# One y visit per group of heads in a Mamba-2 layer, y kept in place of x, and a gate's half moved

## The chip, the cores and the metric

The kernel runs on one core of a Trainium2 chip. Its engines work in parallel, each through its own queue in order: PE (TensorE, matrix products into PSUM), ACT (ScalarE), DVE (VectorE), POOL (GpSimd) and SP (SyncE), which here only starts transfers (DMA). The metric is the device time of one execution in microseconds (us). The kernel before takes 1143.02 us, the median of three runs (1142.99, 1143.02 and 1146.43).

## The reference

The program is a two-layer decoder trunk on 256 positions of width 2048, in float32: a Mamba-2 layer (64 heads of 64 channels in 8 groups, state 128), shared keys and values, an attention layer, and norms. The change is in the Mamba-2 layer, cut to what matters:

```
z, xbc, dt = split(rmsnorm(x) @ w_in)              # xbc: x (4096), B (1024), C (1024)
x, B, C    = split(silu(conv4(xbc)))
dt         = softplus(dt + dt_bias);  a = dt * -exp(A_log)
decay      = exp(cumsum(a)[l] - cumsum(a)[s])  for s <= l      # per head
y          = (C B^T * decay) @ (x * dt)            # per head; C B^T per group
y          = y + D * x
out        = grouped_rmsnorm(y * silu(z)) @ w_out  # 8 groups of 512 channels
```

The sequence is one chunk of 256, so the state that is carried on is never read. After it come `kv = rmsnorm(x) @ w_kv`, 16 attention heads with rope and a causal softmax, and the last two projections.

## The kernel before, in words

All weights are used once. A *unit* is two slices of 128 input channels by 512 output columns of one weight (512 KB). SP loads it (`load`, L292), ACT rounds it to `hi`, DVE subtracts to get `lo` (`split`, L311), and PE multiplies it in `products` (L343) with activations that are split in the same way: for each of two halves of the 256 positions and each of two slices, three large products of 512 columns into a bank `ps`. That is 12 large products a unit and 4,624 in the program, 16 of them for dt. Loads run four units ahead, hi and lo three. `ORDER` (L34) is the order of the blocks of 512 columns: B, C, x and z of the input projection, `o` and `p` of the output projection. The attention layer's blocks follow.

Everything else is *side work*: Python generators that issue a few instructions and yield a condition or a time. After every few large products, `some` (L250, L154) lets generators go on whose inputs, by the planner's own clock (`Paced`, `Clock`, with a cost for each instruction), have been ready for `MARGIN` = 750 ns. So the position of a side product in PE's stream is fixed when the program is built. All instructions of PE, ACT and DVE are issued through one helper line, L126; in the profile they are told apart by tile names. Side products go to four banks `s`. I call a run of side products between two large ones a *visit*.

For a group g of 8 heads (4 head pairs, 512 channels):

- `x_evac` (L805) takes the finished x block out of PSUM. `turn` (L376) scales it by the row factor r0 on ACT, transposes it in 32x32 blocks on DVE into `T`, writes it to DRAM (`turned`, SP) and reads it back with channels in rows into `U` (four reads, POOL).
- `conv_gen` (L621) makes the convolved x in `xs` (12 DVE products, ACT's tanh) and, transposed by PE and multiplied by dt, `xd`.
- `pair_gen(g, j)` (L692), one for each pair j, takes an `em` tile, loads two rows of cumulative sums into all partitions (POOL, 256 KB, L698), makes the decay (ACT) and multiplies by the group's C B^T in `cb` (DVE). There are two `em` tiles. The generator of an odd pair then multiplies pairs j-1 and j on PE in one visit: per pair, four products of xd with em, two heads into the two halves of the bank's rows, so each uses 64 of PE's 128 columns. Each pair's generator then makes `yt` = D xs + q on DVE and multiplies it by 0.5 and by the gate z.
- `z_gen` (L783) makes z (1 + tanh(z/2)) from the turned z block, which was scaled by r0.
- `norm_gen` (L745) waits for the group's four pairs, makes the group's norm (ACT squares, two PE transposes, DVE) and the operand `yn` of the output projection.

Of the kernel before, what the change touches and what calls it, by code (L numbers as in the profile page):

```python
# [9 lines left out]
F32 = mybir.dt.float32  # L10
F32R = mybir.dt.float32r
I32 = mybir.dt.int32
AF = mybir.ActivationFunctionType
OP = mybir.AluOpType

P = 128
L = 256
# [152 lines left out]
def trunk_kernel(ctx: ExitStack, tc: tile.TileContext, x, a_norm_g, a_w_in, a_conv_w, a_conv_b,  # L170
# [3 lines left out]
    clock = Clock()  # L174
# [22 lines left out]
    PE = Paced(clock, nc.tensor, pe_cost, 0.0)  # L197
# [4 lines left out]
    def dram(t, offset, ap):  # L202
# [6 lines left out]
    psum = ctx.enter_context(tc.tile_pool(name="psum", bufs=1, space=bass.MemoryType.PSUM))  # L209
    scratch = ExitStack()  # L210
    work = scratch.enter_context(tc.tile_pool(name="ssd", bufs=2, reuse_waits="tile"))
    S = [Slots(work, {"T": ([P, 512], 2), "u": ([P, 4, L], 1), "xs": ([P, 4, L], 3), "xd": ([P, 2, 512], 1),
                      "cb": ([P, 384], 4), "em": ([P, 2, 384], 2), "z": ([P, 1024], 1), "yt": ([P, 4, L], 2)})]
    banks = Slots(psum, {"s": ([P, 512], 8 - MAIN_BANKS)}, clock.banks)
    spare = Parts(big, "U", "y5", [P, 1024], 2)
    B = {}
# [4 lines left out]
    def of(tag):  # L221
        return next(s for s in (banks, S[0], spare) if tag in s.shape)

    def can(*tags):
        return lambda: all(of(t).free(t) > 0 for t in tags)

    def take(tag):
        return of(tag).take(tag)
# [3 lines left out]
    def give(*tiles):  # L232

        for t in tiles:
            key = t.tensor.name, t.offset
            freed.append((next(s for s in (banks, S[0], spare) if key in s.held), key, clock.last))

# [163 lines left out]
    def by_channel(U):  # L401

        return U.rearrange("p (b j l) -> p j b l", b=8, j=4)
# [2 lines left out]
        return a.rearrange("p j (b l) -> p j b l", l=32)  # L406


    ga = const.tile([16, P], F32, name="ga")
    SP.dma_start(ga, dram(a_norm_g, 0, [[P, 16], [1, P]]))  # L410
    xl = [big.tile([P, D], F32, name=f"xl{t}", tag=f"y{4 + t}") for t in range(2)]
    xv = x[0].rearrange("(t p) d -> p t d", p=P)
# [53 lines left out]
    def root(t, count):  # L466

        v, h, y, a = (t[:, i, :] for i in range(4))
        DVE.tensor_scalar(v, v, 1.0 / count, EPS, op0=OP.mult, op1=OP.add)
        ACT.activation(h, v, AF.Sqrt)  # L470
        DVE.reciprocal(y, h)
        DVE.tensor_mul(a, y, y)
        DVE.tensor_mul(a, a, v)
        DVE.tensor_scalar(a, a, -0.5, 1.5, op0=OP.mult, op1=OP.add)
        DVE.tensor_mul(y, y, a)
# [22 lines left out]
    warm_up()  # L498
    nt = const.tile([P, 4, 2], F32, name="r0")
    r0 = nt[:, 2, :]  # L500

    def squares(h):

# [4 lines left out]
    def first_norm():  # L508
        DVE.tensor_reduce(nt[:, 0, :], ss, axis=mybir.AxisListType.X, op=OP.add)
        root(nt, D)  # L510

    gv = const.tile([P, 112], F32, name="gv")
    cbias = const.tile([P, 48], F32, name="cbias")
# [34 lines left out]
    st = {}  # L548
# [28 lines left out]
    def dt_gen(w):  # L577
        u, m, e, s, s2 = (w[0:64, i, :] for i in range(5))
        DVE.scalar_tensor_tensor(m, u, -1.0, u, op0=OP.mult, op1=OP.min)
        yield  # L580
        ACT.activation(e, m, AF.Exp)
        yield
        DVE.tensor_scalar(m, e, 2.0, None, op0=OP.add)
        DVE.reciprocal(s2, m)
        DVE.tensor_mul(s, e, s2)
        yield
        DVE.tensor_mul(s2, s, s)
        DVE.tensor_scalar(m, s2, 1.0 / 17, None, op0=OP.mult)
        for n in range(7, 0, -1):
            DVE.scalar_tensor_tensor(m, m, 1.0 / (2 * n + 1), s2, op0=OP.add, op1=OP.mult)  # L590
            if n % 2:
                yield
        DVE.scalar_tensor_tensor(m, m, 1.0, s, op0=OP.add, op1=OP.mult)
        DVE.tensor_scalar(e, u, 0.0, None, op0=OP.max)
        dt = s2
        DVE.scalar_tensor_tensor(dt, m, 2.0, e, op0=OP.mult, op1=OP.add)
        yield
        a, b = m, e
        DVE.tensor_scalar(b, dt, negA, None, op0=OP.mult)
        POOL.memset(u, 1.0)  # L600
        yield
        DVE.tensor_tensor_scan(a, u, b, 0.0, OP.mult, OP.add)
        yield
        AC = hbm.tile([64, L], F32, name="AC")
        POOL.dma_start(AC, a)
        st["AC"] = AC
        b = w[:, 2, :]
        DVE.tensor_copy(b[64:128, :], a)
        DVE.tensor_copy(b[0:64, :], dt)
        yield DVE.ns + 3000.0  # L610
        yield can("s")
        p = take("s")[:, :L].rearrange("p (t c) -> p t c", t=2)
        for t in range(2):
            PE.transpose(p[:, t, :], b[:, t * P:(t + 1) * P], ident)
        yield
        dal = const.tile([P, 2, P], F32, name="dal", tag="c2")
        ACT.activation(dal, p, AF.Copy)
        give(p)
        st["dal"] = dal
# [69 lines left out]
                side.add(cb_gen(q), lambda: ("B", q) in st and ("C", q) in st)  # L689
        return evac  # L690

    def pair_gen(g, j):  # L692

        c = 4 * g + j
        E = take("em")
        AC = st["AC"]
        R = bass.AP(tensor=AC.tensor, offset=AC.offset + 2 * c * L, ap=[[0, P], [L, 2], [1, L]])
        POOL.dma_start(E[:, :, :L], R)  # L698
        yield copied(E)
        yield lambda: "dal" in st  # L700
        dal = st["dal"]
        for h in range(2):
            a = 64 + 2 * c + h
            ACT.activation(E[:, h, 256:384], E[:, h, P:L], AF.Relu, bias=dal[:, 1, a:a + 1], scale=-1.0)
            ACT.activation(E[:, h, 0:256], E[:, h, 0:256], AF.Relu, bias=dal[:, 0, a:a + 1], scale=-1.0)
        ACT.activation(E, E, AF.Exp, scale=-1.0)
        yield lambda: ("cb", g) in st
        DVE.tensor_mul(E, E, st["cb", g][:, None, :].to_broadcast([P, 2, 384]))
        st["em", g, j], when["em", g, j] = E, clock.last
        if j % 2:  # L710
            yield lambda: ("xd", g) in st and ("em", g, j - 1) in st
            yield max(when["xd", g], when["em", g, j - 1])
            yield lambda: of("s").free("s") > 1 and (("y", g) in st or can("yt")())
            for i in (j - 1, j):
                xd, E, q = st["xd", g], st.pop(("em", g, i)), take("s")[:, :L]
                for h in range(2):
                    PE.matmul(q[h * 64:(h + 1) * 64, :], lhsT=xd[:, 0, i * P + h * 64:i * P + (h + 1) * 64],
                              rhs=E[:, h, 0:256], start=True, stop=False)
                for h in range(2):
                    PE.matmul(q[h * 64:(h + 1) * 64, P:L], lhsT=xd[:, 1, i * P + h * 64:i * P + (h + 1) * 64],  # L720
                              rhs=E[:, h, 256:384], start=False, stop=True)
                give(E)
                st["q", g, i], when["q", g, i] = q, clock.last
            if ("y", g) not in st:
                st["y", g], st["n", g] = take("yt"), 0
            yield
        else:
            yield lambda: ("q", g, j) in st
            yield when["q", g, j]
        xd, xs, q = st["xd", g], st["xs", g], st.pop(("q", g, j))  # L730
        y = st["y", g][:, j, :]
        DVE.scalar_tensor_tensor(y, xs[:, j, :], Dv[:, c:c + 1], q, op0=OP.mult, op1=OP.add)
        give(q)
        st["x", g] = st.get(("x", g), 0) + 1
        if st["x", g] == 4:
            give(xs, xd, st["cb", g])
        yield lambda: ("z", g) in st
        z = st["z", g]
        y = y.rearrange("p (b l) -> p b l", l=32)
        DVE.scalar_tensor_tensor(y, y, 0.5, by_channel(z)[:, j], op0=OP.mult, op1=OP.mult)  # L740
        st["n", g] += 1
        if st["n", g] == 4 and g not in (1, 3):
            give(z)

    def norm_gen(g):  # L745
# [37 lines left out]
    def z_gen(U, there, g):  # L783

        yield there
        if g in (1, 3):
            yield lambda: g == 1 or st.get(("n", 1)) == 4
            z = big.tile([P, 1024], F32, name=f"z{g}", tag="y4")
        else:
            yield can("z")  # L790
            z = take("z")
        ACT.activation(z, U, AF.Tanh, scale=0.5)
        yield
        DVE.scalar_tensor_tensor(z, z, 1.0, U, op0=OP.add, op1=OP.mult)
        give(U)
        st["z", g] = z

    def z_evac(g):
        def evac(ps, t):
            U, there = turn(ps, t, r0)  # L800
            if t:
                side.add(z_gen(U, there, g))
        return evac

    def x_evac(g):  # L805
        base = conv_evac(4 * g, ("xs", g), g)

        def evac(ps, t):
            base(ps, t)
            if not t:  # L810
                return
            for j in range(4):
                side.add(pair_gen(g, j), lambda: "AC" in st and can("em")())
            side.add(norm_gen(g), lambda: st.get(("n", g)) == 4)
        return evac

# [66 lines left out]
    def r1_gen():  # L883
# [16 lines left out]
        ACT.activation(rB, R, AF.Copy)  # L900
        give(R)
        yield
        csr = const.tile([P, 2, L], F32, name="csr", tag="c2")
        DVE.tensor_mul(csr, B["cs"], rB[:, None, :].to_broadcast([P, 2, L]))
        B["csr"] = csr
        bop = [big.tile([P, 4, 2 * L], F32R, name=f"bop{i}", tag=f"y{i}") for i in range(4)]
# [341 lines left out]
```

## Time and profile before

| | |
|---|---|
| median of the runs | 1143.02 us |
| profiled execution, its own time | 1143.61 us |
| its span, first to last instruction | 1141.9 us |
| PE busy | 1130.1 us, 99%, 5217 instructions |
| DVE busy | 839.2 us, 73%, 1283 instructions |
| ACT busy | 641.6 us, 56%, 890 instructions |
| POOL busy | 124.4 us, 11%, 217 instructions |
| HBM traffic | 226 GB/s over the span |

Shares are of the span. Matmuls are pipelined: the recorded time of one overlaps the next, so PE's rate is read from starts and not from durations. A wait is told as the engine that waited, the tile that it worked for, and what ended the wait. An fp32 side product is recorded as two instructions (two passes); a large product, whose operands are rounded, as one.

### The profile page before, as it was taken

How to read it: one execution, taken by the hardware profiler on the slowest of the kernel's cores; microseconds unless marked ns; L12 is line 12 of the kernel's file. 1: busy time of each engine (PE TensorE's matmuls, PEld its weight loads, DVE VectorE, ACT ScalarE, POOL GpSimd, SP SyncE). 2: the span in 40 equal slices, each digit the busy share in tenths (PEclk: the TensorE clock that was granted, in tenths of full speed). 3: DMA queues.
4: the chain of work that ended last, by engine and by line, in shares of the span. 5: the costliest groups of instructions: out<-in, count | busy, mean ns of one | idle time of the engine just before them, and what ended most of it. 6: DMA issues, size and time to landing. Idle time of an engine off the chain costs nothing.

```text
span 1141.9 us, 14900 instructions
## 1 busy us (share of the span) xinstructions
PE 1130.1 (99%) x5217; PEld 923.2 (81%) x5217; DVE 839.2 (73%) x1283; ACT 641.6 (56%) x890; POOL 124.4 (11%) x217
## 2 busy tenths in 40 slices
PE   9999999999999999999999999999999999999996
PEld 6888888888888888888878888888888888888885
DVE  5787878778799878787877558876445597887564
ACT  5666566767656666667554655434343444445353
POOL 2011112012011111101000000000000012122000
PEclk9999999999999999999999999999999999999998
DMA  8787888878778777777765467768658688888852
GB/s 263 222 242 242 249 229 278 268 243 253 210 222 240 223 237 225 237 234 231 215 232 177 162 197 218 224 200 261 220 174 244 209 248 237 263 250 261 254 185 92
DMA packets 130363, 258.91 MB, mean 227 GB/s; under 512 B 12976, under 2 KB 13824, under 8 KB 129904
## 3 DMA queue, kind: packets, MB, share of 16 engines
q1 hardware_dynamic: 119232, 226.01, 63.2%
q0 software_dynamic: 11056, 31.95, 10.9%
q8 instruction: 41, 0.67, 0.2%
q14 instruction: 34, 0.28, 0.1%
HBM read 235.83 MB, written 22.09 MB: 226 GB/s over the span
## 4 chain that ended last, share of the span: by engine, by line
PE 96%; DMA 1%; DVE 1%; ACT 0%; SPq 0%; issue 0%; ACTq 0%; DVEq 0%
PE ps L126 90%; PE s L126 6%; DMA raw<-in_a_w_in_dram 1%; PE ps_dt L126 0%; DVE xs L126 0%; DVE lo L126 0%; ACT hi L126 0%; SPq L416 0%; DVE x L126 0%; DVE T L126 0%; SPq L306 0%; ACT T L126 0%; ACT x L126 0%; DVE sfin L126 0%; ACTq L1243 0%
## 5 line engine op out<-in xcount | busy, mean ns | idle before, releaser
L126 DVE TENSOR_TENSOR lo<-raw,hi 128x1024 fp32r<-128x1024 f32 (+1 forms) x385 | 462.7, 1215 | 192.1 <-ACT hi L126 189.1
L126 ACT ACTIVATE hi<-raw 128x1024 fp32r<-128x1024 f32 (+1 forms) x385 | 397.7, 1052 | 263.3 <-PE ps L126 137.5
L126 PE MATMUL ps<-hi,hT 128*128 128x512 f32 x1280 | 401.1, 394 | 0.5 <-ACT hi L126 0.4
L126 PEld LDWEIGHTS ps<-hi,hT 128*128 128x128 f32 x1280 | 235.6, 188 | 49.2 <-issue 2.1
L126 PE MATMUL ps<-lo,hT 128*128 128x512 f32 x640 | 249.8, 390 | 0.0
L126 PE MATMUL ps<-hi,bop 128*128 128x512 f32 x512 | 161.1, 396 | 0.0
L126 PE MATMUL ps<-hi,yn 128*128 128x512 f32 x512 | 159.7, 393 | 0.0
L126 PE MATMUL ps<-hi,kvop 128*128 128x512 f32 x512 | 158.2, 390 | 0.0
L397 POOL DMA_DIRECT2D U<-turned x128 | 74.3, 587 | 748.9 <-DMA turned<-T 408.2
L126 PEld LDWEIGHTS ps<-lo,hT 128*128 128x128 f32 x640 | 120.1, 188 | 26.4 <-DVE lo L126 0.9
L126 PEld LDWEIGHTS ps<-hi,kvop 128*128 128x128 f32 x512 | 95.7, 188 | 19.7
L126 PEld LDWEIGHTS ps<-hi,bop 128*128 128x128 f32 x512 | 95.8, 188 | 19.4
L126 PEld LDWEIGHTS ps<-hi,yn 128*128 128x128 f32 x512 | 94.7, 188 | 19.4 <-issue 0.5
L126 PE MATMUL ps<-lo,yn 128*128 128x512 f32 x256 | 99.8, 390 | 0.0
L126 PE MATMUL ps<-lo,bop 128*128 128x512 f32 x256 | 99.8, 390 | 0.0
L126 PE MATMUL ps<-lo,kvop 128*128 128x512 f32 x256 | 99.7, 389 | 0.0
L126 PE MATMUL ps<-hi,oop 128*128 128x512 f32 x256 | 78.9, 390 | 0.0
L126 DVE STREAM_TRANSPOSE T<-ps 128x512 f32<-128x512 f32 x64 | 43.4, 699 | 25.6 <-ACT ps L126 15.9
L126 DVE SCALAR_TENSOR_TENSOR xs<-u,cw,xs 128x255 f32<-128x255 f32 (+2 forms) x144 | 59.7, 475 | 0.0
L126 ACT ACTIVATE em<-em,dal 128x128 f32<-128x128 f32 (+1 forms) x128 | 54.4, 449 | 5.0 <-DMA em<-AC 2.9
L126 PEld LDWEIGHTS ps<-lo,bop 128*128 128x128 f32 x256 | 48.0, 188 | 10.3
L126 PEld LDWEIGHTS ps<-lo,yn 128*128 128x128 f32 x256 | 48.0, 188 | 10.1
(165 smaller groups left out, 922.5 us busy)
## 6 DMA issues: line engine op xcount, KB each, us to landing
raw<-in_a_w_in_dram SPq DMA_DIRECT2D x159, 512.0 KB, 5.3
raw<-in_a_w_out_dram SPq DMA_DIRECT2D x64, 512.0 KB, 4.8
raw<-in_w_kv_dram SPq DMA_DIRECT2D x64, 512.0 KB, 4.8
raw<-in_b_w_in_dram SPq DMA_DIRECT2D x64, 512.0 KB, 4.7
turned<-T SPq DMA_DIRECT2D x64, 256.0 KB, 4.3
U<-turned POOLq DMA_DIRECT2D x128, 128.0 KB, 6.5
raw<-in_b_w_out_dram SPq DMA_DIRECT2D x32, 512.0 KB, 4.9
em<-AC POOLq DMA_DIRECT2D x32, 256.0 KB, 6.0
```

Source lines behind the costliest of these rows:

```text
L126: return call(out, *args, **kw)
L397: POOL.dma_start(U[32 * q:32 * q + 32].rearrange("p (b c) -> p b c", b=8), src)
```

## The change

`pair_gen` is cut in two. `em_gen(g, j)` makes one pair's em tile; `y_gen(g)` waits for xd and all four em tiles and issues the products of all four pairs in one visit, two pairs to a bank, side by side. y is then written over the group's xs, so `yt` is gone, and its room goes to a fourth xs and two more em tiles (four in all). The product with z is done for two pairs at once and without the factor 0.5; that factor is now in r0h = r0/2, by which z is scaled when it leaves PSUM, and z's tanh loses its scale of 0.5. Three small tiles change places.

```diff
-    S = [Slots(work, {"T": ([P, 512], 2), "u": ([P, 4, L], 1), "xs": ([P, 4, L], 3), "xd": ([P, 2, 512], 1),
-                      "cb": ([P, 384], 4), "em": ([P, 2, 384], 2), "z": ([P, 1024], 1), "yt": ([P, 4, L], 2)})]
+    S = [Slots(work, {"T": ([P, 512], 2), "u": ([P, 4, L], 1), "xs": ([P, 4, L], 4), "xd": ([P, 2, 512], 1),
+                      "cb": ([P, 384], 4), "em": ([P, 2, 384], 4), "z": ([P, 1024], 1)})]
...
+        DVE.tensor_scalar(r0h, r0, 0.5, None, op0=OP.mult)
...
-    def pair_gen(g, j):
+    def em_gen(g, j):
...
         DVE.tensor_mul(E, E, st["cb", g][:, None, :].to_broadcast([P, 2, 384]))
         st["em", g, j], when["em", g, j] = E, clock.last
-        if j % 2:
-            yield lambda: ("xd", g) in st and ("em", g, j - 1) in st
-            yield max(when["xd", g], when["em", g, j - 1])
-            yield lambda: of("s").free("s") > 1 and (("y", g) in st or can("yt")())
-            for i in (j - 1, j):
-                xd, E, q = st["xd", g], st.pop(("em", g, i)), take("s")[:, :L]
+        st["ems", g] = st.get(("ems", g), 0) + 1
+        if st["ems", g] == 4:
+            give(st["cb", g])
+
+    def y_gen(g):
+
+        yield lambda: ("xd", g) in st and st.get(("ems", g)) == 4
+        yield max(when["xd", g], *(when["em", g, j] for j in range(4)))
+        yield lambda: of("s").free("s") > 1
+        xd, y = st["xd", g], st["xs", g]
+        Q = []
+        for i in (0, 2):
+            q = take("s").rearrange("p (j l) -> p j l", j=2)
+            Q.append(q)
+            for j in (i, i + 1):
+                E = st.pop(("em", g, j))
                 for h in range(2):
-                    PE.matmul(q[h * 64:(h + 1) * 64, :], lhsT=xd[:, 0, i * P + h * 64:i * P + (h + 1) * 64],
+                    PE.matmul(q[h * 64:(h + 1) * 64, j - i, :], lhsT=xd[:, 0, j * P + h * 64:j * P + (h + 1) * 64],
                               rhs=E[:, h, 0:256], start=True, stop=False)
                 for h in range(2):
-                    PE.matmul(q[h * 64:(h + 1) * 64, P:L], lhsT=xd[:, 1, i * P + h * 64:i * P + (h + 1) * 64],
+                    PE.matmul(q[h * 64:(h + 1) * 64, j - i, P:L], lhsT=xd[:, 1, j * P + h * 64:j * P + (h + 1) * 64],
                               rhs=E[:, h, 256:384], start=False, stop=True)
                 give(E)
...
-        y = st["y", g][:, j, :]
-        DVE.scalar_tensor_tensor(y, xs[:, j, :], Dv[:, c:c + 1], q, op0=OP.mult, op1=OP.add)
...
+        give(xd)
+        for i in (0, 2):
+            yield
+            for j in (i, i + 1):
+                c = 4 * g + j
+                DVE.scalar_tensor_tensor(y[:, j, :], y[:, j, :], Dv[:, c:c + 1], Q[i // 2][:, j - i, :],
+                                         op0=OP.mult, op1=OP.add)
+            give(Q[i // 2])
         yield lambda: ("z", g) in st
         z = st["z", g]
-        y = y.rearrange("p (b l) -> p b l", l=32)
-        DVE.scalar_tensor_tensor(y, y, 0.5, by_channel(z)[:, j], op0=OP.mult, op1=OP.mult)
...
+        for i in (0, 2):
+            v = y[:, i:i + 2, :].rearrange("p j (b l) -> p j b l", l=32)
+            DVE.tensor_mul(v, v, by_channel(z)[:, i:i + 2])
+            yield
...
-        ACT.activation(z, U, AF.Tanh, scale=0.5)
+        ACT.activation(z, U, AF.Tanh)
...
-            U, there = turn(ps, t, r0)
+            U, there = turn(ps, t, r0h)
...
             for j in range(4):
-                side.add(pair_gen(g, j), lambda: "AC" in st and can("em")())
+                side.add(em_gen(g, j), lambda: "AC" in st and can("em")())
+            side.add(y_gen(g))
...
-        csr = const.tile([P, 2, L], F32, name="csr", tag="c2")
+        csr = p.tile([P, 2, L], F32, name="csr", bufs=1)
```

How the program's order changes is seen at three places. On PE, around the first y visit of the first group (s is the side bank, 64x256 and 64x128 are a head's two products), before:

```order
L126 MATMUL ps<-hi,hT 128x512 x2
L126 MATMUL ps<-lo,hT 128x512
L126 MATMUL s<-em,xd 64x256 x2
L126 MATMUL s<-em,xd 64x128 x2
L126 MATMUL s<-em,xd 64x256 x2
L126 MATMUL s<-em,xd 64x128 x2
L126 MATMUL ps<-hi,hT 128x512 x2
L126 MATMUL ps<-lo,hT 128x512
```

and on PE at the same place now:

```order
L126 MATMUL ps<-hi,hT 128x512 x2
L126 MATMUL ps<-lo,hT 128x512
L126 MATMUL s<-em,xd 64x256 x2
L126 MATMUL s<-em,xd 64x128 x2
L126 MATMUL s<-em,xd 64x256 x2
L126 MATMUL s<-em,xd 64x128 x2
L126 MATMUL s<-em,xd 64x256 x2
L126 MATMUL s<-em,xd 64x128 x2
L126 MATMUL s<-em,xd 64x256 x2
L126 MATMUL s<-em,xd 64x128 x2
L126 MATMUL ps<-hi,hT 128x512 x2
L126 MATMUL ps<-lo,hT 128x512
```

Four rows, two pairs, have joined the visit; the group's second visit, further on, is gone. On POOL, in the middle of the Mamba-2 layer (U are the four reads that turn a block, em the loads of a pair), before:

```order
L397 DMA U<-turned 32x8x128 x8
L698 DMA em<-AC 128x2x256 x2
L397 DMA U<-turned 32x8x128 x4
L698 DMA em<-AC 128x2x256 x2
L397 DMA U<-turned 32x8x128 x4
L698 DMA em<-AC 128x2x256 x2
```

and on POOL now:

```order
L700 DMA em<-AC 128x2x256 x4
L397 DMA U<-turned 32x8x128 x12
L700 DMA em<-AC 128x2x256 x4
L397 DMA U<-turned 32x8x128 x12
L700 DMA em<-AC 128x2x256 x4
```

A group's four loads now follow each other. On DVE, the longest stretch between two subtractions that make a lo, in the Mamba-2 layer (cb and squares are named above; the yt rows are two pairs' y), before:

```order
L126 TENSOR_TENSOR lo<-raw,hi 128x1024 x2
L126 SCALAR_TENSOR_TENSOR yt<-xs,Dv,s 128x256 x2
L126 SCALAR_TENSOR_TENSOR yt<-yt,z_2439 128x256 x2
L126 TENSOR_TENSOR cb<-s,tri 128x384
L126 TENSOR_TENSOR squares<-squares 128x512
L126 TENSOR_TENSOR squares<-squares 128x256
L126 TENSOR_TENSOR lo<-raw,hi 128x1024
```

and on DVE the longest one now (the xs rows are the convolution's products, nt a norm's two columns):

```order
L126 TENSOR_TENSOR lo<-raw,hi 128x1024
L126 TENSOR_TENSOR nt_2479<-nt_2479 128x2
L126 SCALAR_TENSOR_TENSOR xs<-u,cw,xs 128x255 x4
L126 SCALAR_TENSOR_TENSOR xs<-u,cw,xs 128x254 x4
L126 TENSOR_TENSOR nt_2479<-nt_2479 128x2
L126 SCALAR_TENSOR_TENSOR nt_2479<-nt_2479 128x2
L126 TENSOR_TENSOR nt_2479<-nt_2479 128x2 x2
L126 SCALAR_TENSOR_TENSOR nt_2479<-nt_2479 128x2
L126 SCALAR_TENSOR_TENSOR xs<-u,cw,xs 128x253 x4
L126 TENSOR_TENSOR lo<-raw,hi 128x1024
```

The whole convolution of a block stands between two of them, where its three rows used to be apart.

## Rows read from the trace of the kernel before

**Rows 1.** The page: PE's busy time, and the chain's shares by line.
```profile
PE 1130.1 (99%) x5217; PEld 923.2 (81%) x5217; DVE 839.2 (73%) x1283; ACT 641.6 (56%) x890; POOL 124.4 (11%) x217
...
PE ps L126 90%; PE s L126 6%; DMA raw<-in_a_w_in_dram 1%; PE ps_dt L126 0%; DVE xs L126 0%; DVE lo L126 0%; ACT hi L126 0%; SPq L416 0%; DVE x L126 0%; DVE T L126 0%; SPq L306 0%; ACT T L126 0%; ACT x L126 0%; DVE sfin L126 0%; ACTq L1243 0%
```
**Rows 2.** The waits of PE: what it waited for, us, times, longest.
```profile
PE s L126 <- DVE early L126: 1.2, 1, 1.2
PE s L126 <- DMA xl<-in_x_dram: 0.5, 1, 0.5
PE ps L126 <- ACT hi L126: 0.4, 1, 0.4
```
**Rows 3.** Windows: us, busy us (instructions) of each engine, clock, DMA share, GB/s.
```profile
140.00:610.00 470.00, 470.00 (x2258) 381.29 (x2258) 377.66 (x603) 308.63 (x415) 58.53 (x95) 1.00 0.78 234
...
200.00:300.00 100.00, 100.00 (x475) 81.36 (x474) 77.64 (x117) 68.36 (x94) 13.54 (x22) 1.00 0.85 251
```
**Rows 4.** PE in order of time around a y visit: start, us, what, count.
```profile
168.86 0.62 PE L126 MATMUL ps<-hi,hT 128*128 128x512 f32 x2
169.32 0.39 PE L126 MATMUL ps<-lo,hT 128*128 128x512 f32 x1
169.63 1.52 PE L126 MATMUL s<-em,xd 128*64 128x256 f32 x16
171.09 0.73 PE L126 MATMUL ps<-hi,hT 128*128 128x512 f32 x2
171.66 0.39 PE L126 MATMUL ps<-lo,hT 128*128 128x512 f32 x1
```
**Rows 5.** PE's weight loads (PEld) inside that visit, one pair apart.
```profile
169.90 0.14 PEld L126 LDWEIGHTS s<-em,xd 128*64 128x64 f32 x2
...
170.55 0.14 PEld L126 LDWEIGHTS s<-em,xd 128*64 128x64 f32 x2
```
**Rows 6.** The chain of waits in order of time, three side visits.
```profile
136.97 0.44 PE s L126 x4
...
140.15 1.45 PE s L126 x16
...
195.97 0.22 PE s L126 x2
```
**Rows 7.** Groups of instructions: shape, count, busy us, mean ns, idle before.
```profile
L126 PE MATMUL s<-em,xd 128*64 128x256 f32 (+1 forms) x256 | 24.3, 332 | 0.0
...
L126 DVE SCALAR_TENSOR_TENSOR yt<-xs,Dv,s 128x256 f32<-128x256 f32 x32 | 14.9, 476 | 8.6 <-PE s L126 8.5
...
L126 DVE SCALAR_TENSOR_TENSOR yt<-yt,z 128x256 f32<-128x256 f32 x32 | 13.1, 419 | 0.2
...
L126 DVE TENSOR_TENSOR K<-U,csr 128x512 f32<-128x512 f32 x8 | 5.5, 693 | 0.1
```
**Rows 8.** The page's DMA issues: the loads of em, size and us to landing.
```profile
em<-AC POOLq DMA_DIRECT2D x32, 256.0 KB, 6.0
```
**Rows 9.** Groups of DVE instructions: convolution, cb and squares.
```profile
L126 DVE SCALAR_TENSOR_TENSOR xs<-u,cw,xs 128x255 f32<-128x255 f32 (+2 forms) x144 | 59.7, 475 | 0.0
...
L126 DVE TENSOR_TENSOR squares<-squares 128x512 f32<-128x512 f32 (+1 forms) x16 | 8.9, 554 | 0.9 <-ACT squares L126 0.7
...
L126 DVE TENSOR_TENSOR cb<-s,tri 128x384 f32<-128x384 f32 x8 | 4.3, 544 | 0.0
```
**Rows 10.** In order of time: one unit's lo on DVE, its use on PE.
```profile
247.79 1.22 DVE L126 TENSOR_TENSOR lo<-raw,hi 128x1024 fp32r<-128x1024 f32 x1 [6.23 <-ACT hi L126]
...
251.92 0.39 PE L126 MATMUL ps<-lo,hT 128*128 128x512 f32 x1
```
**Rows 11.** The weight tiles raw: their loads from issue to landing.
```profile
DMA to landing us min/median/max: 3.5/4.9/13.0
```

More of the change, by code (lines that the diff above doesn't have):

```diff
@@ L406, in in_32s @@
         return a.rearrange("p j (b l) -> p j b l", l=32)
-    ga = const.tile([16, P], F32, name="ga")
+    ga = const.tile([16, P], F32, name="ga", tag="c1")
     SP.dma_start(ga, dram(a_norm_g, 0, [[P, 16], [1, P]]))
@@ L500, in trunk_kernel @@
     r0 = nt[:, 2, :]
+    r0h = const.tile([P, 2], F32, name="r0h")
     def squares(h):
@@ L615, in dt_gen @@
         yield
-        dal = const.tile([P, 2, P], F32, name="dal", tag="c2")
+        dal = const.tile([P, 2, P], F32, name="dal", tag="c1")
         ACT.activation(dal, p, AF.Copy)
@@ L718, in pair_gen @@
                               rhs=E[:, h, 0:256], start=True, stop=False)
                 for h in range(2):
-                    PE.matmul(q[h * 64:(h + 1) * 64, P:L], lhsT=xd[:, 1, i * P + h * 64:i * P + (h + 1) * 64],
+                    PE.matmul(q[h * 64:(h + 1) * 64, j - i, P:L], lhsT=xd[:, 1, j * P + h * 64:j * P + (h + 1) * 64],
                               rhs=E[:, h, 256:384], start=False, stop=True)
                 give(E)
-                st["q", g, i], when["q", g, i] = q, clock.last
@@ L724, in pair_gen @@
-            if ("y", g) not in st:
-                st["y", g], st["n", g] = take("yt"), 0
+        give(xd)
+        for i in (0, 2):
             yield
[L727 to L730, printed above, removed]
-        y = st["y", g][:, j, :]
-        DVE.scalar_tensor_tensor(y, xs[:, j, :], Dv[:, c:c + 1], q, op0=OP.mult, op1=OP.add)
-        give(q)
-        st["x", g] = st.get(("x", g), 0) + 1
@@ L735, in pair_gen @@
-        if st["x", g] == 4:
-            give(xs, xd, st["cb", g])
+            for j in (i, i + 1):
[3 more added lines that the diff above has]
+            give(Q[i // 2])
         yield lambda: ("z", g) in st
         z = st["z", g]
-        y = y.rearrange("p (b l) -> p b l", l=32)
-        DVE.scalar_tensor_tensor(y, y, 0.5, by_channel(z)[:, j], op0=OP.mult, op1=OP.mult)
@@ L741, in pair_gen @@
-        st["n", g] += 1
-        if st["n", g] == 4 and g not in (1, 3):
+        for i in (0, 2):
+            v = y[:, i:i + 2, :].rearrange("p j (b l) -> p j b l", l=32)
+            DVE.tensor_mul(v, v, by_channel(z)[:, i:i + 2])
+            yield
+        st["y", g] = y
+        st["n", g] = 4
+        if g not in (1, 3):
             give(z)
```

## The prediction

> **What bounds the kernel now.** I read the page first. TensorE (PE) is busy 99% of the span, and in the chain of work that ended last the large products into ps hold 90% and the side products into s 6% [rows 1]. The list of waits then says how much idling of PE somebody ended: three waits, 2.1 us together, on tiles of the first microseconds [rows 2]. [...] What counts is PE's own work: its instructions, and the time between them that the busy figure hides because matmuls overlap.
>
> So I looked at PE's order of time around one y visit. In an undisturbed group of three large products the third starts 0.46 us after the first (168.86 to 169.32), which is 0.23 us a product. Behind the product at 169.32 the y products start at 169.63, 0.31 later and not 0.23; the next large product starts at 171.09, and the third of its group 0.57 and not 0.46 us after it [rows 4]. The visit costs 171.09 - 169.32 - 0.23 = 1.54 us, and the group behind it loses 0.11: 1.65 us.
>
> How much of that is products? The visit's 16 recorded instructions are two passes of each of eight products; the two heads of a pair run side by side. Weight loads exactly one pair apart start at 169.90 and 170.55, on either side of the border between the visit's two pairs: 0.65 us a pair, border included [rows 5]. Two pairs are 1.30 us. So 1.65 - 1.30 = 0.35 us of each visit is coming and going: 0.08 ahead of its first pass, 0.11 in the large products behind it, and the rest in its first and last passes.
>
> That is not the price of any side visit. In the chain a visit of two transposes (recorded as four) stands with 0.44 us and a visit of one with 0.22: nothing is paid for coming and going [rows 6]. The y products differ from these in that they use the array in two halves of 64 columns (the form 128*64). [...]
>
> **The change part by part.**
>
> *One visit for four pairs.* Before, the odd pair's generator multiplies two pairs, so 8 groups have 16 visits; the group row counts 256 instructions, 16 x 16 [rows 7], and the first of the 16 stands in the chain with 1.45 us [rows 6]. After, each group has one visit, eight rows of the order with no large product between them. The products are the same in number, shape and operands; only half of the result bank differs. Eight entries and exits go: 8 x 0.35 = 2.8 us less on PE, which is the path. Two side visits that were shared stand apart now (squares beside transposes of xs, and a y visit beside a cb product), so of 107 visits 101 stay and not 99. Visits of transposes or of cb products use all 128 columns and pay nothing for coming and going; I take 0 for these, between -0.1 and +0.2 us.
>
> Can the longer visit stall inside? All four E tiles, xd and two banks are required before it is placed, and it is placed 750 ns of the planner's time behind them, as the short ones are. The border between two pairs, with its change of E tile and of bank, exists today inside every visit and costs nothing [rows 5]; now there are three such borders. Bounds: 0 to 0.35 us per visit, the whole saving; I take 0, the nearest row.
>
> *y in place of xs, and the product with z.* Per group DVE had four products with z of 0.419 us and has two of twice the width; the nearest row is the 128x512 product at 0.693 us [rows 7]. That is 8 x (4 x 0.419 - 2 x 0.693) = 2.3 us less of DVE. The factor 0.5 goes into r0h, one more instruction on two columns, once, with no wait of PE behind it [rows 2]. The gate's tanh loses a constant scale. The rope table csr gets a tile of its own in a stage where PE's order stays as it is. All of these lie beside a PE that is never idle: 0. If that cover were gone, DVE's 2.3 us would be a gain, so the bound lies below nothing.
>
> *When y is ready.* The second visit of a group used to come after 661, 889, 1153, 1420, 1669, 1909, 2149 and 2383 of the program's 4,624 large products; the one visit comes after 556, 748, 964, 1189, 1576, 1876, 2056 and 2344. Every group's y, and what is made of it, comes earlier, so no reader of it can be the new wait.
>
> *What the new buffers move.* With four em tiles POOL issues the four loads of a group in a row, where they come as twos today (x4 in the order where x2 was). Two tiles more in a burst are 2 x 256 KB [rows 8], and at the 251 GB/s of a full stretch [rows 3] that is 2.1 us of all DMA engines. DVE's stream also gets a longer stretch between two subtractions that make a lo: twelve convolution products of 0.475 us, 5.7 us without the six two-column ones among them, where the longest today is 2 x 0.476 + 2 x 0.419 + 0.544 + 2 x 0.554 = 3.4 us [rows 7, 9]: 2.3 more. Both can make a lo late. Of the 202 weight units used between 100 and 695 us, the one with the least reserve has its lo done at 247.79 + 1.22 = 249.01 and used at 251.92: 2.9 us [rows 10]. Either delay alone fits in the least reserve there is; I take 0. Together they miss it by 2.1 + 2.3 - 2.9 = 1.5 us, so the other bound is 7 refills x 1.5 = 10.5 us. Weight loads already take 3.5 to 13.0 us to land [rows 11] with no wait of PE on them in this stage [rows 2].
>
> [...]
>
> **The sum.** -2.8 us. The profiled execution took 1143.61 us, of which the span is 1141.9 and 1.7 lies around it; it would take 1140.8. The median of the runs shown, 1143.02, is 0.6 below that execution, so the median goes to **1140.2 us**, 0.25% less. I call 0.3% (3.4 us) what a measurement of this kernel can tell from no change; the likeliest result is a real gain just inside it. With 0.05 us of doubt in each 0.35 (0.4 us for eight) and the 0.6 us between profiled run and median, the case's own range is 1139.2 to 1141.2.
>
> **Rivals.**
> - *The gain is lost inside.* The long visit waits for a late E tile or bank, or one stall of some 3 us eats the saving. For: company saves nothing for transposes, 0.44 us for two and 0.22 for one [rows 6]. Against: those have no ends to save, and the y products' borders are seen to be free [rows 5]. Time 1143.0 us.
> - *Slower: the weights come late.* One mechanism: right behind a y visit the burst of four em loads delays the weights, and a long DVE stretch falls on the same units, so lo misses its reserve and PE waits 1.5 us at each such refill. It shows as slower from 3.4 + 2.8 = 6.2 us of stalls, five of the seven refills. With all seven: 1143.0 - 2.8 + 10.5 = 1150.7 us. For: the DMA engines are 0.85 busy between 200 and 300 us [rows 3], where the least reserve is. Against: it needs both delays on the unit with the least reserve, again and again.
>
> **How the numbers follow.** Forecast 0.76, gain lost 0.16, slower 0.08. The forecast's own range lies across the bound of 1139.6 (0.3% under 1143.0), with about a third of it on the far side: faster 0.26, within 0.3% 0.50 + 0.16 = 0.66, slower 0.08. The range of 8 in 10 goes from 1138.9, a little under the forecast's own, to 1143.4, which takes in the lost gain and leaves out the slower case.
>
> **What would show it.** In the profile after, PE has the same 5217 instructions, with a busy time near 1127 us. The chain shows eight y visits of 32 recorded instructions and some 1.45 + 1.30 = 2.75 us, and none of 16. PE's lead over the old trace grows by 0.35 us a group, is complete by 610 us and constant after it. DVE's busy time falls by about 2 us, without effect. The prediction is wrong if a y visit takes 2 x 1.45 us or more, if PE waits for hi or lo between 100 and 640 us by more than 0.5 us, or if the lead after 610 us is not about 2.8 us.

## The result, and the profile after

The changed kernel takes **1148.43 us** (median of 8 runs, 1147.37 to 1154.66) where the kernel before takes 1143.01 (8 runs): 1.0052 times as long, 95% interval 1.0037 to 1.0067 (such a ratio is made from all runs, and is not exactly that of the two medians). The prediction, 1140.2 and at most 1143.4, was wrong, in sign too.

Its own step came out as priced. In the page, PE's instructions are the same in number and its busy time is 2.2 us less than in [rows 1]:

```profile
PE 1127.9 (98%) x5217; PEld 923.8 (81%) x5217; DVE 836.0 (73%) x1268; ACT 639.5 (56%) x890; POOL 127.0 (11%) x217
```

Around the first y visit, in PE's order of time (columns as in [rows 4]), the visit of 32 stands where 16 stood:

```profile
145.16 0.39 PE L126 MATMUL ps<-lo,hT 128*128 128x512 f32 x1
145.47 2.82 PE L126 MATMUL s<-em,xd 128*64 128x256 f32 x32
148.22 0.73 PE L126 MATMUL ps<-hi,hT 128*128 128x512 f32 x2
148.80 0.39 PE L126 MATMUL ps<-lo,hT 128*128 128x512 f32 x1
```

148.22 - 145.16 - 0.23 = 2.83 us and 0.12 in the group behind: 2.95, which is 4 x 0.65 + 0.35. So 2.8 us were saved; but the span is 1146.6 us and not 1141.9, so something took 4.7 + 2.8 = 7.5. The list of PE's waits says what. With one more line of 0.2 us, for hT, it makes 9.3 us, where the three lines of before [rows 2] made 2.1; 7.2 are new:

```profile
PE s L126 <- DVE xs L126: 2.9, 2, 1.5
PE ps L126 <- DVE lo L126: 1.9, 1, 1.9
PE s L126 <- DVE early L126: 1.2, 1, 1.2
PE s L126 <- DMA xl<-in_x_dram: 0.7, 1, 0.7
PE s L126 <- DVE nt L126: 0.7, 1, 0.7
PE ps L126 <- ACT hi L126: 0.6, 1, 0.6
PE s L126 <- DVE squares L126: 0.6, 1, 0.6
PE s L126 <- DMA Es<-turned_E: 0.5, 1, 0.5
```

xs, nt and squares are inputs of side visits in the Mamba-2 layer; the lo is one of the K and V projection behind it, and Es belongs to the attention, stages whose PE order the change leaves as it was. The window of [rows 3] now has PE busy 467.30 of 470 us:

```profile
140.00:610.00 470.00, 467.30 (x2256) 381.32 (x2255) 379.04 (x594) 304.17 (x407) 61.61 (x97) 1.00 0.78 233
```

and in the page's DMA issues the em loads of [rows 8] land 2.6 us later:

```profile
em<-AC POOLq DMA_DIRECT2D x32, 256.0 KB, 8.6
```

How such a wait comes about is seen at 456 us. In the kernel before, DVE finishes that xs 2.27 us before PE transposes it (start, us, what; DVE's line, then PE's):

```profile
442.18 1.22 DVE L126 SCALAR_TENSOR_TENSOR xs<-u,xs 128x1024 f32<-128x1024 f32 x1
...
445.67 0.60 PE L126 MATMUL s<-ident,xs 128*128 128x128 f32 x4
```

In the changed kernel, in DVE's order of time (in brackets the idle time before and what ended it):

```profile
451.06 0.95 DVE L126 TENSOR_TENSOR em<-em,cb 128x768 f32<-128x768 f32 x1
454.64 2.36 DVE L126 TENSOR_TENSOR lo<-raw,hi 128x1024 fp32r<-128x1024 f32 x2 [2.62 <-ACT hi L126]
456.91 1.22 DVE L126 SCALAR_TENSOR_TENSOR xs<-u,xs 128x1024 f32<-128x1024 f32 x1
```

and in PE's:

```profile
456.48 0.39 PE L126 MATMUL ps<-lo,hT 128*128 128x512 f32 x1
458.28 0.63 PE L126 MATMUL s<-ident,xs 128*128 128x128 f32 x4 [1.41 <-DVE xs L126]
```

The u for this xs is done on ACT at 450.04 + 1.06 = 451.10 us, but DVE does not take the product ahead of the two los in front of it: it stands 2.62 us at a lo whose hi is late, and starts the product at 456.91. In the chain of waits that hi starts when its weight has landed, 5.06 us after the issue (until then ACT is busy with an em as well):

```profile
448.46 5.06 DMA raw<-in_a_w_out_dram
...
453.56 1.05 ACT hi L126
```

PE does not wait for the lo itself; but the product into xs is queued behind it, and the four transposes of xs on PE were placed close behind that product. So here a late weight is paid for by a side visit, not by the product that uses the weight. In the projection it is the other way round. DVE there in the kernel before:

```profile
782.60 1.39 DVE L126 TENSOR_TENSOR T<-U,csr 64x512 f32<-64x512 f32 x2 [2.07 <-DMA U<-turned]
...
788.17 4.62 DVE L126 TENSOR_TENSOR lo<-raw,hi 128x1024 fp32r<-128x1024 f32 x4
```

and in the changed kernel, with PE's wait behind it:

```profile
787.22 1.39 DVE L126 TENSOR_TENSOR T<-U,csr 64x512 f32<-64x512 f32 x2 [2.64 <-DMA U<-turned]
...
792.79 3.49 DVE L126 TENSOR_TENSOR lo<-raw,hi 128x1024 fp32r<-128x1024 f32 x3
...
794.07 0.50 PE L126 MATMUL ps<-lo,kvop 128*128 128x512 f32 x1 [1.94 <-DVE lo L126]
```

The four U loads of this turn are issued from 776.12 us and the last lands 9.3 us after its issue; before, from 773.74 and 7.1 us. DVE starts 4.6 us later, 2.4 of them already late at the issue, and PE waits 1.9 us for the lo behind.

### The profile page after: what moved, and what is told of

The parts are those of the page before. It is cut to its first block, busy times and chain, and to the rows that moved or that the text cites. A ratio compares the mean times of both kernels' runs of the same rounds, so it can differ in the third digit from the quotient of the medians.

```text
span 1146.6 us, 14871 instructions
## 1 busy us (share of the span) xinstructions
PE 1127.9 (98%) x5217; PEld 923.8 (81%) x5217; DVE 836.0 (73%) x1268; ACT 639.5 (56%) x890; POOL 127.0 (11%) x217
## 3 DMA queue, kind: packets, MB, share of 16 engines
q0 software_dynamic: 11056, 31.95, 11.1%
## 4 chain that ended last, share of the span: by engine, by line
PE 80%; DMA 8%; DVE 6%; issue 2%; ACT 2%; POOL 0%; SPq 0%; ACTq 0%; DVEq 0%; POOLq 0%
PE ps L126 75%; PE s L126 5%; DMA raw<-in_a_w_in_dram 4%; DVE lo L126 3%; DVE xs L126 2%; DMA U<-turned 1%; ACT hi L126 1%; DVE T L126 1%; DMA turned<-T 1%; DMA Es<-turned_E 1%; DMA raw<-in_a_w_out_dram 0%; POOL U L397 0%; DVE x L126 0%; ACT xs L126 0%; ACT u L126 0%
## 5 line engine op out<-in xcount | busy, mean ns | idle before, releaser
L126 PEld LDWEIGHTS ps<-hi,bop 128*128 128x128 f32 x512 | 95.8, 188 | 19.6
L126 PEld LDWEIGHTS ps<-hi,kvop 128*128 128x128 f32 x512 | 95.7, 188 | 19.6
L126 PEld LDWEIGHTS ps<-lo,kvop 128*128 128x128 f32 x256 | 48.0, 188 | 12.5 <-DVE lo L126 2.4
L126 PEld LDWEIGHTS ps<-hi,oop 128*128 128x128 f32 x256 | 47.9, 188 | 9.8
```

The source lines that it names most:

```text
L126: return call(out, *args, **kw)
```

## The experiments

Times are medians; ratios are to the kernel before on the same chip, with the 95% interval. Two theories came first: that the burst of four em loads delays the others, and that the planner places side visits too close behind their inputs.

**Loads paced, and held back.** The em loads two by two (first line), and the burst only behind the reads of U (second):

```
+ side.add(em_gen(g, j), lambda j=j: ... st["ems", g] >= j - 1 if j > 1 else g == 0 or st["taken", g - 1] == 4)
...
+ side.add(em_gen(g, j), lambda: "AC" in st and ("turned", g) in st and can("em")())
```

> The changed kernel, with the four em loads of a group issued two by two: the third and fourth pair wait until the first and second have their em tile finished. The visit of four pairs stays. Theory burst (four em loads in a row slow weights and turned blocks, ACT stands in order behind them, DVE's side work comes late and PE's side visits wait): em loads land in about 6.1 us again instead of 8.3, weight loads near them in about 5.9 instead of 8.5, PE's waits between 90 and 690 us fall from about 5 us to under 1 us, and the time goes to about 1141 (1140 to 1142.5). Rival margin (long stretches of DVE work and a planner's margin of 750 ns are the cause, whatever the loads do): 1146 to 1149. Rival other (buffers' places, the row factor): 1146 to 1149.

> The changed kernel, with the burst of four em loads of a group issued only after the group's turned x block U has been read by ACT; the loads stay four in a row. Theory burst by way of U (what hurts is that the em loads follow right behind U's reads on POOL's queue, so that U lands late and ACT stands at it): ACT's waits for U of 4.5 to 6.7 us go, the time falls to about 1141 to 1143, although the em loads still land in about 8 us. Theory burst by way of the weights (what hurts is that the weights land late): little changes, 1145 to 1149. Rival margin: 1145 to 1149.

Measured: 1150.35 (1.0057, 1.0042 to 1.0073) and 1147.89 (1.0050, 1.0032 to 1.0068). em still lands in 8.3 and 8.4 us by the page (8.6 in the changed kernel), in twos as well. So four in a row in the order of issue isn't it. A late landing is not tested by these two, for they did not bring it down.

**The planner's numbers.** READ from 7000 to 9000, and MARGIN from 750 to 2000:

> The changed kernel, where the planner reckons 9 us and not 7 us from the issue of a POOL load to its landing, so that ACT's read of a turned block and the work on em stand later in ACT's stream; loads stay four in a row. Theory burst by way of U: ACT's waits for U shrink by about 2 us each and with them PE's waits: 1141 to 1144. Rival margin: the long DVE stretches stay, 1145 to 1149. Rival other: 1146 to 1149.

> The changed kernel with the planner's margin for side work raised from 750 to 2000 ns, so that every side product stands further behind its inputs in PE's stream; loads stay four in a row. Theory burst: PE's waits for side inputs (0.8 to 1.6 us each, four in the layer) mostly go, since the side inputs are late by about that, but waits for lo stay where weights are late: 1141 to 1145. Rival margin: all of the layer's waits go, 1140 to 1142. Rival other: 1146 to 1149.

1148.09 (1.0041, 1.0029 to 1.0053) and 1150.44 (1.0065, 1.0043 to 1.0087). Neither helps; with the larger margin the larger waits stand in the attention and the projection instead.

**Where the tiles lie.** What was left were edits priced at nothing. The new tile r0h takes 32 bytes of each partition among the constants, and every pool behind them has moved (the tiles that changed places move them by a multiple of 256 more). Counted in 256 bytes, weights, stage buffers and the Mamba-2 scratch tiles begin 192 over a multiple before, and 224 over after. Columns that nothing uses move them alone:

```
- ones = const.tile([P, 2], F32, name="ones")
+ ones = const.tile([P, 10], F32, name="ones")    # 32 bytes; 18: 64; 26: 96
```

> The changed kernel with eight unused columns more in the small constant tile ones (2 to 10): every tile of the pools behind the constants moves up by 32 bytes, so that the tiles which transfers write (raw, em, U, T, Es) begin at a multiple of 64 bytes of their partition again, as in the kernel before; in the changed kernel they all begin 32 bytes off one. Nothing else differs. Theory alignment: transfers land as before (em near 6 us where the changed kernel's take 8.3, raw between the y visits 5.9 instead of 8.5), PE's waits of 1 to 2 us go, and the 2.8 us of the merged visits are left: 1140.2 (1139.5 to 1141.5). Rival places and burst (more buffers, other order of the loads): nothing changes, 1147 to 1150.

> The kernel before with the same eight columns: here they move the tiles behind the constants from a multiple of 64 bytes to 32 bytes off one; visits, buffers and orders are those of before. Theory alignment: em lands in 8 us or more, raw near the visits in 8.5, PE waits for xs, lo and Es as in the changed kernel, and the time is that of the changed kernel plus the 2.8 us of the visits that were not merged, less what the smaller bursts spare: 1146 to 1152. Rival: 1143, as before.

> Control: the kernel before with sixteen columns more in ones: the tiles behind it move by 64 bytes and stay at multiples of 64. Theory alignment: 1143.0 (1142.3 to 1144). If any move of the addresses costs time, or the larger tile does: 1146 or more.

> The changed kernel with everything behind the constants moved up by 96 bytes and not by 32: tiles begin at multiples of 64 that are not multiples of 128, as in the kernel before. Theory that 32 bytes off a multiple of 64 is what costs: 1143 to 1144.5, near the version moved by 32 (1143.06), whose tiles are at multiples of 128. Rival, that only multiples of 128 are good and any other place costs the changed kernel 5 us: 1147 to 1149.

| start of the tiles, over a multiple of 256 | kernel before | changed kernel |
|---|---|---|
| 0 | 1143.67 (0.9995, 0.9985 to 1.0005) | 1143.06 (0.9990, 0.9980 to 0.9999) |
| 192, and 64 for the changed one | 1143.69 (23 runs) | 1147.64 (1.0033, 1.0020 to 1.0045) |
| 224 | 1148.10 (1.0033, 1.0018 to 1.0047) | 1148.43 (1.0052, 1.0037 to 1.0067) |

The place alone gives the changed kernel 5.4 us back, and costs the kernel before 4.4. In the same row the two kernels differ by 0.6 us at 0, hardly more than the scatter of the runs, and by 0.3 at 224, which the scatter doesn't tell from none. But the last run refutes half of the theory: 64 over, at a multiple of 64 like the 192 of the kernel before, the changed kernel is still 3.9 us slower than that kernel. Whether the kernel before bears such a place better, or 192 is a better place than 64, stays open: no run has the changed kernel at 192. (The expectations speak of 64 and 128. All the good places are multiples of 256 too; no run tells 128 from 256. The attention's own tiles begin elsewhere: its U 64 over and its Es 64 and 128 over in the row of 0; 0 over, and 0 and 64, in the kernel before.)

The pages show the transfers. POOL's queue (U, em, Es), its packets, MB and their time as a share of 16 engines' span: in the changed kernel,

```profile
q0 software_dynamic: 11056, 31.95, 11.1%
```

in the same kernel at multiples of 256,

```profile
q0 software_dynamic: 11056, 31.95, 10.1%
```

and in the kernel before at multiples of 256:

```profile
q0 software_dynamic: 11056, 31.95, 10.5%
```

The kernel before as it was has 10.9%. In the changed kernel the same packets take a tenth less: 0.101 x 1141.5 x 16 / 11056 = 167 ns each, and 184 after. By size, the 4096-byte ones take 239 ns (changed, 0 over), 246 (before, 0 over), 258 (before), 264 (changed, 64 over), 266 (after) and 267 (before, 224 over); the 256-byte packets of the dt weights take 17.9 ns in all runs whose raw tiles begin at a multiple of 256, and 18.8 to 19.6 in all others. The tile's own place counts: packets that start while only em loads are under way take 159 to 165 ns in the median in every run whose em tiles begin at a multiple of 256, and 174 to 187 in every other, whatever the places of the rest. The engines' own work hardly changes with the place: the kernel before has DVE busy 839.2 us at 192 and 838.7 at 224, ACT 641.6 and 641.2, and its large products stand 227 ns apart at both.

By the means above, the 4096-byte packets take 5 to 11% more off a multiple of 256 than in the same kernel at one. The bulk of the weights does not show it: their 108,032 packets of 2048 bytes take 84 ns in the median at every place, and 102 to 104 in the mean with raw at a multiple of 256 against 103 to 105 elsewhere. Why the place counts for the ones and hardly for the others is shown by no run.

**Which tiles.** Only the scratch pools 32 bytes further; and raw 32 bytes further, in a pool of its own behind lo (the scratch pools then begin at a multiple of 256, where all else stays at 192 over):

```
+ wts.tile([P, 8], F32, name="pad", tag="pad", bufs=1)      # behind lo
...
+ rawp.tile([P, 8], F32, name="lead", tag="lead", bufs=1)   # ahead of raw, and a second behind it
```

> The kernel before with an unused tile of 32 bytes behind the weights: only the tiles of the two scratch pools (em, T, xs, u, cb, U of the attention, Es, PT) move, to 32 bytes off a multiple of 64; raw, hi, lo and the large stage buffers stay where they were. Theory transfers of the scratch tiles: most of the loss of the kernel that moved everything, 1146 to 1149. Rival, that the weights' tiles are what counts (raw written by SP's loads, hi and lo read by PE): 1143 to 1144.

> The kernel before with raw in a pool of its own behind lo, 32 bytes off a multiple of 64; hi and lo lie 16384 bytes lower, so that they and hT still begin at the same offset within 4096 bytes, and the scratch pools move by 64. In the earlier raw run that distance between hi and hT had changed by 64 bytes, and PE's large products stood 229 ns apart and not 227, which is what it measured. Theory, the weights' loads hold what the scratch pools (1.7 of 4.6 us) leave: 1145 to 1147, products 227 ns apart. Rival, raw's place costs nothing: 1143 to 1144.

1145.03 (1.0020, 1.0009 to 1.0031) and 1144.90 (1.0009, 0.9998 to 1.0019). Scratch costs 1.7 of the 4.4 us; raw about 1.2, which isn't told from nothing. Neither pool alone holds the loss.

**A detour: PE's operands.** Unused bytes that part the weights from the rest, in the same manner: raw, hi and lo off by 32 bytes; the stage buffers alone off by 32; raw off by 32, with hi and lo moved by 64; and the same with the scratch pools off by 32 too. All else lies at multiples of 64.

> The kernel before with 32 unused bytes ahead of the weights and 32 behind them: only raw, hi and lo lie 32 bytes off a multiple of 64; the scratch pools move by 64 and stay aligned. Theory scratch tiles: 1143 to 1144. Rival weights: 1146 to 1149. If both this and the other kernel of the pair lose half each (1145 to 1146), every transfer pays.

> The kernel before with only the stage buffers (hT, yn, kvop, bop, oop and x) 32 bytes off a multiple of 64; raw, hi, lo and the scratch pools aligned. The weights alone off cost 26 us: PE's large products stood 234 ns apart and not 227, while with everything off they stand 227 apart. If the two operands of a product must lie alike, the products stand 234 apart here too and the time is 1165 to 1170. If it is the weights' own place: 227 and 1143 to 1146.

> The kernel before with 32 unused bytes ahead of the raw tiles and 32 more behind them: only raw, which SP's loads write and ACT and DVE read, lies 32 bytes off a multiple of 64; hi, lo, hT and everything else are aligned. Theory transfers: raw lands later (5.5 us or more where the aligned control has 5.2) and part of the 4.6 us that the move of everything cost is seen: 1144.5 to 1147. Rival, that PE's operands are what costs: 1143.3, and PE's large products stay 227 ns apart.

> As the run before, and the scratch pools (em, T, xs, U, Es) 32 bytes off as well; hi, lo, hT and the stage buffers aligned. Theory transfers: the whole loss of the kernel that moved everything, 1147 to 1149. Rival, that the stage buffers or PE's operands hold part of it: 1145, as the scratch pools alone.

1169.27 (1.0225, 1.0212 to 1.0239), 1171.04 (one run), 1152.29 (1.0066, 1.0054 to 1.0079), 1151.66 (1.0066, 1.0053 to 1.0080). No new wait stands behind these; PE itself is slower. In the pages of the first three:

```profile
PE 1156.2 (99%) x5217; PEld 922.5 (79%) x5217; DVE 842.6 (72%) x1283; ACT 642.7 (55%) x890; POOL 124.2 (11%) x217
```

```profile
PE 1156.6 (99%) x5217; PEld 922.4 (79%) x5217; DVE 841.5 (72%) x1283; ACT 642.0 (55%) x890; POOL 124.4 (11%) x217
```

```profile
PE 1139.3 (99%) x5217; PEld 924.7 (80%) x5217; DVE 840.0 (73%) x1283; ACT 641.6 (56%) x890; POOL 124.2 (11%) x217
```

against 1130.1 before [rows 1]. Large products start 234 ns apart where hi and hT are 32 bytes out of step and 229 where they are 64 out, against 227 where their distance is a multiple of 4096 (medians of 4,624). So the last two runs say nothing of transfers. In the changed kernel that distance is as before: this is not its cause.

**What the visits are worth, and the rest.** At multiples of 256, the changed kernel with its visit cut in two (a yield between the pairs):

> The changed kernel at aligned places (as the first kernel of this call), but with its y visit cut into two of 16 products each, as before the change: 16 visits instead of 8. Theory alignment with the predicted price of a visit: 8 x 0.35 = 2.8 us over the first kernel of this call, 1143.0. Rival, that the merged visits save nothing of the time: as the first kernel.

1144.73 (1.0005, 0.9996 to 1.0015), 1.7 us over the same kernel uncut: of 2.8 us priced, 1.7 show in the time. The cut also makes the planner place the visits elsewhere, and PE waits less, 2.8 us for 3.5. In the two profiles the spans are 1143.7 and 1141.5 us: 2.2 and the 0.7 less of waits make 2.9, which is the price. And three ways to get the rest, paced loads, MARGIN 1500, and MARGIN 1500 in the Mamba-2 layer alone:

> The changed kernel at aligned places (1143.06) with its em loads two by two and held until the group before has been multiplied. Theory that what is left of the loss comes from the burst of four loads: em lands in 6 us again and the time is 1140.2 to 1141.5. Rival, that it comes from DVE's work in longer pieces (xs, squares and nt late by 0.2 to 0.9 us): 1142.5 to 1143.5.

> The changed kernel at aligned places with the planner's margin at 1500 ns and not 750: a side visit is placed that much later behind its inputs. Theory DVE's longer pieces: the waits for xs, squares and nt go (about 1.9 us in the profile of the aligned kernel) and the time is 1141 to 1142. Rival burst, or that the later visits only move the waits to the attention: 1143 or more.

> The changed kernel at aligned places, with the planner's margin at 1500 ns up to the end of the Mamba-2 layer and at 750 behind it. Theory that the rest of the loss is waits of side visits for DVE's longer pieces (xs, squares, nt; 1.9 us more than before in the aligned kernel's profile): these waits go and the time is 1140.5 to 1142. Rival, that later visits make others late: 1143 to 1146.

1143.59 (1.0006, 0.9994 to 1.0017), 1150.34 (1.0057, 1.0043 to 1.0071), 1144.10 (0.9997, 0.9988 to 1.0006). None does. In the last, the waits for xs and squares are gone, and nt (1.5 us) and Es (1.9) stand in their place. The waits of PE, whole margin at 1500:

```profile
PE s L126 <- DMA Es<-turned_E: 3.1, 2, 2.9
PE ps L126 <- ACT oop L126: 1.4, 1, 1.4
PE s L126 <- DVE nt L126: 1.1, 2, 0.8
```

That a visit placed later makes its own readers late fits these waits; no run shows it by itself. The version at multiples of 256 is the best of all (1143.06), by 0.1% of the kernel before. Its waits of PE:

```profile
PE s L126 <- DVE early L126: 1.2, 1, 1.2
PE s L126 <- DVE xs L126: 0.9, 2, 0.6
PE s L126 <- DVE squares L126: 0.6, 1, 0.6
PE s L126 <- DMA Es<-turned_E: 0.3, 1, 0.3
PE s L126 <- DMA xl<-in_x_dram: 0.3, 1, 0.3
PE ps L126 <- ACT hi L126: 0.2, 1, 0.2
```

xs, squares and Es, 1.8 us, are what is new against the kernel before [rows 2]; of the 2.8 saved about 0.6 is left in the medians against that kernel at the same places. Pacing does bring em's landing down here, from 7.6 to 6.8 us, without a gain.

## Why the prediction was wrong

The forecast missed by 1148.43 - 1140.2 = 8.2 us. Two terms that it put at nothing make that up: 5.4 us that go when the tiles are put back to multiples of 256, and 2.9 that stay there (1143.06 - 1140.2).

- *What bounds the kernel*, *one visit for four pairs*, *no stall inside*: right. The visit costs 2.95 us in the trace; seven of the eight stand in the chain with 2.75. Why a y visit pays at its ends is not shown. That a visit of cb products doesn't is seen in the kernel before: of the seven that stand alone, in the form 128*128, six start 0.23 us behind the large product ahead of them, a large product's own step, where the y visits start 0.32 behind. One reading on the way is wrong without effect: a transpose is recorded once and not twice, so 0.44 us [rows 6] are four transposes and 0.22 are two, still 0.11 each and nothing for coming and going.
- *y in place*: right; DVE's busy time fell by 3.2 us, without effect.
- *"Every group's y ... comes earlier, so no reader of it can be the new wait"*: wrong. Its readers are placed earlier too, as close behind as the planner allows. nt waits 0.7 us and squares 0.6.
- ***"Either delay alone fits in the least reserve there is; I take 0"*: one step that failed, 2.9 us.** I looked for the least reserve among the weights alone. There it held, if barely: no product between 100 and 640 us waits for a hi or lo, but the least reserve of a lo between 100 and 695 us went from 2.9 us to 0.45 (1.70 at multiples of 256). The thin reserves are those of the side visits. From the end of DVE's input to the start of the visit the least for a transpose of xs is 2.27 us before and 0.15 after, for a y visit 1.39 and 0.09, for nt 0.77 and 0.15; where PE waits for DVE, 0.15 is what is left. At the two other places the changed kernel has 0.15 for xs as well, and the kernel before at 224 over still has 2.26: it is the new order, not the place. The burst's own delay was priced well: at multiples of 256 em lands in 7.6 us, for 5.5 in the kernel before at the same places, 2.1 later; with r0h's place it is 8.6 for 6.0. That xs, squares and Es make up the 2.9 is read from one profile, in which they are 1.8; no run took them away without others in their place.
- ***"All of these lie beside a PE that is never idle: 0"*, of r0h and csr: the other step that failed, and the larger one, 5.4 us.** Their instructions do lie beside it. That r0h's 32 bytes move every tile behind was not thought of. That the place costs is shown: 5.4 us come back when it alone is changed, and the kernel before, with nothing changed but the place, loses 4.4 at 224 over. That the loss needs both, a late transfer and a thin reserve of the new order, is not shown: the kernel before has its old reserves and loses about as much. Where its loss stands is seen in its profile: PE is 1.0 us behind the old trace when the Mamba-2 layer ends and 5.8 at the end, most of it from one wait in the attention (below), which the change leaves as it was.
- *"PE's lead over the old trace"*, the prediction's own test: at the 2,600th large product, behind the last visit, the changed kernel is not 2.8 us ahead but 1.8 behind; the projection takes 2.3 more and the attention 0.7. At multiples of 256 it is 1.2 ahead there.
- *Rival "the weights come late"*, at 8 in 100: near in size, 1150.7, and wrong in mechanism. That the bounds of the delays, 0 to 10.5 us, hold the 7.5 is luck, for the larger part has another cause. *Rival "the gain is lost inside"*: no.

What stays open: how the loss divides over single tiles; what the changed kernel does at 192 over; and why pacing does not cure the later em landing at 224.

## What to carry to other kernels

When PE is 99% busy, price each change of order at the inputs of the side work, not only at the weights: take the least time from the end of a producer to its consumer, for every kind of visit, and ask what stands ahead of that producer on its engine. A new small tile moves all that is allocated behind it. Before you judge a change of less than 1%, put the large tiles of both kernels to the same places and time them again; in these runs multiples of 256 bytes were the best for both.

## What was not expected of the hardware

- Transfers into tiles that begin off a multiple of 256 bytes: POOL's 4096-byte packets took 239 to 247 ns in the runs that have all of weights, stage buffers and Mamba-2 scratch tiles at one, and 256 to 281 in all others.
- A product's two operands: 32 bytes out of step in their partitions cost 7 ns of 227 a product in the median, 26 and 27 us in all.
- One wait cost 1.7 times its length. In the kernel before at 224 over, PE waits 2.06 us for Es; then the granted clock is 0.50, and large products start 0.43 us apart until 1073 us. PE in order of time:

```profile
1066.07 0.39 PE L126 MATMUL ps<-lo,oop 128*128 128x512 f32 x1
1068.52 1.77 PE L126 MATMUL s<-Es,V 128*128 128x256 f32 x8 [2.06 <-DMA Es<-turned_E]
1069.94 1.20 PE L126 MATMUL ps<-hi,oop 128*128 128x512 f32 x2
1070.94 0.63 PE L126 MATMUL ps<-lo,oop 128*128 128x512 f32 x1
1071.37 1.05 PE L126 MATMUL ps<-hi,oop 128*128 128x512 f32 x2
```

and the windows behind it (the clock is the third figure from the end):

```profile
1070.00:1073.00 3.00, 3.00 (x9) 2.40 (x8) 3.00 (x5) 1.77 (x3) 0.00 (x0) 0.50 1.03 384
1074.00:1078.00 4.00, 4.00 (x19) 3.29 (x18) 2.05 (x2) 1.06 (x1) 0.00 (x0) 1.00 0.71 242
```

The visit itself takes 1.42 us to its next product, the wait 2.06, and the seven products behind lose some 0.2 us each: 1.4 us more. Another wait of nearly that length, the 1.94 us that end at 794 us in the changed kernel, has the granted clock at 1.00 behind it, from 794 to 800 us.
